# A hybrid attention and convolution layer on one core: sixteen convolution blocks regrouped as Strassen products ahead of the attention

## The chip, the core and the metric

The kernel runs on one core of one Trainium2 chip. TensorE does the matmuls, VectorE, ScalarE and GpSimd do the elementwise work, and SyncE issues nearly all transfers. In the rows these are PE, DVE, ACT, POOL and SP; PEld is the weight load of PE. The metric is the device time of one execution in microseconds, as the median of several runs; one profiled execution gives the rows.

## What is computed

One decoder layer in float32, 1024 positions and 16 learned meta positions ahead of them, width 1024. A normalised input is projected to 4104 columns; half of them feed softmax attention, the other half a gated convolution of width 3; both branches are normalised per head or group, gated, and go through one output projection.

```python
def _hybrid_layer(h, norm_g, w_in, b_f, conv_w, attn_norm_g, conv_norm_g, w_out):
    u = _rmsnorm(h, norm_g)
    proj = jnp.einsum('bld,de->ble', u, w_in)
    q, k, v, f_logit, z_attn, gate_b, gate_c, xc, z_conv = jnp.split(proj, SPLIT_POINTS, axis=-1)
    log_f = jax.nn.log_sigmoid(f_logit + b_f)
    cum_logf = jnp.cumsum(log_f, axis=1)
    attn = _fox_attention(q.reshape(shp), k.reshape(shp), v.reshape(shp), cum_logf)
    y_attn = _group_rmsnorm(attn, attn_norm_g, ATTN_HEADS) * jax.nn.silu(z_attn)
    conv = _causal_depthwise_conv(gate_c * xc, conv_w)
    y_conv = _group_rmsnorm(gate_b * conv, conv_norm_g, CONV_GROUPS) * jax.nn.silu(z_conv)
    mix = jnp.concatenate([y_attn, y_conv], axis=-1)
    return h + jnp.einsum('ble,ed->bld', mix, w_out)
```

The attention has 8 heads of 64 and a causal mask; its logits are q.k/8 plus the difference of the summed log forget gates. A last normalisation follows the layer.

## The kernel before

**Numbers in two parts.** Each float32 operand of a large matmul is held as a rounded part `hi` and the rest `lo`, and each product is three matmuls: hi by hi, lo by hi, hi by lo. To split a tensor takes one copy (ScalarE, or GpSimd for weights in `hi_pool`, L112) and one subtraction (VectorE, `lo_vec`, L115).

**Input and q (L211 to L250).** Eight row tiles of the transposed input `xs` and of the q weights are loaded, split, and multiplied for the four q blocks at once (L232, 192 matmuls of 512 columns into eight PSUM tiles). The input isn't normalised over its tokens first: only the gain `gnt` is applied. The factor of each token, `rbc`, is found beside this from a second load of the input (`ht`, L249, squares on ScalarE) and is multiplied in wherever a projection leaves PSUM (L275, L297, L451, L472, L478 and so on).

**k and v (L165, L324).** Two k blocks, then v with the forget gate (L324, 260 columns a matmul, two PSUM tiles for each of nine token tiles), then two k blocks. A block is 128 output columns: 8 input tiles by 3 matmuls for each chunk of positions. q, k and v go to DRAM in parts and come back head by head (`load_head`).

**Filler and attention.** The 16 convolution blocks (gates c, x, b and zc in four groups) and the four z gates of the attention are cut into steps of three matmuls, in the list `filler`. The attention is cut into stages, one for each head and half of its queries: `s_step` (scores, row maximum on VectorE, exponential on ScalarE), `s_end` (the small chain of GpSimd, ScalarE and VectorE that merges the maxima, then the scaling of the probabilities `pn` on GpSimd, L635), `t_step` (transposes on TensorE, copy `ph` on ScalarE, subtraction `pl` on VectorE), `v_step` (L669) and `fold`. While a stage transposes and multiplies one half, it already does the scores of the next. `weave` sets TensorE's order: it puts filler steps between the attention's, in proportion to the matmul time left, with a start of `HEAD` us of filler before the first scores. Every matmul of this part is `pinned` to that order; the other engines' order is chosen by the compiler's scheduler.

**Finish.** `norm` and `silu` finish a branch; the output projection (L788, 360 matmuls, most of 512 columns) reads the branches back from DRAM (`yd`), adds the input and applies the last norm.

Of the kernel before, what the change touches and what calls it, by code (L numbers as in the profile page):

```python
# [22 lines left out]
KT = 8  # L23
# [12 lines left out]
def hybrid_kernel(ctx, tc, hT, h, w_q, w_vf, w_m, w_o, gn, bf, cw, ga, gc, gf, out):  # L36
# [37 lines left out]
    rtok = const.tile([P, 9], F32, name="rtok")  # L74
    rbc = const.tile([P, L], F32, name="rbc")
    r2bc = const.tile([P, L], F32, name="r2bc")

# [18 lines left out]
    FIN = (4, 12)  # L96
    FIN3 = (8, 1)
# [21 lines left out]
    wp = xctx.enter_context(tc.tile_pool(name="wp", bufs=2, side=R_SIDE))  # L119
# [6 lines left out]
    order = [0, 1, 2, 3]  # L126
    for i in range(4):
        order += [4 + 4 * i, 5 + 4 * i, 7 + 4 * i] + ([20 + i, 6 + 4 * i] if i < 3 else [6 + 4 * i, 20 + i])
    staged, ready = {}, {}

    def load_w(m):
        staged[m] = wp.tile([P, KT, P], F32, name="wm", bufs=1)
        ins = nc.sync.dma_start(staged[m], w_m[m].rearrange("p (k c) -> p k c", k=KT))
        if m < 4:
            behind(ins)

    def split_w(m):
        ws = staged.pop(m)
        whi = wp.tile([P, KT, P], F32R, name="wmhi")
        wlo = wp.tile([P, KT, P], F32R, name="wmlo")  # L140
        hi_pool(whi, ws)
        lo_vec(wlo, ws, whi)
        ready[m] = whi, wlo

    def block_steps(m, chunks, psum, done):

        at = order.index(m)
        nxt = order[at + 1] if at + 1 < len(order) else None
# [28 lines left out]


    with ExitStack() as ca:
# [3 lines left out]
        kp = ca.enter_context(tc.tile_pool(name="kp", bufs=2))  # L183
        qk = ca.enter_context(tc.tile_pool(name="qk", bufs=1))
        st = ca.enter_context(tc.tile_pool(name="st", bufs=2))
        sm = ca.enter_context(tc.tile_pool(name="sm", bufs=1))

        ones = sm.tile([P, P], F32, name="ones")
        nc.gpsimd.memset(ones, 1.0)
        tri = sm.tile([P, P], F32, name="tri")  # L190
# [6 lines left out]
        nc.vector.tensor_copy(blk, blk32)  # L197

# [4 lines left out]
        for i in range(8):  # L203
            nc.tensor.matmul(pw, zero[:, :P], zero, start=True, stop=True)


        psq = [[(psx if (m, c) == (3, 1) else ps1).tile([P, 512], F32, name="px" if (m, c) == (3, 1) else "ps")
                for c in range(2)] for m in range(4)]
        with ExitStack() as c1:
            wq = c1.enter_context(tc.tile_pool(name="wq", bufs=3))  # L210
            for k in range(KT):  # L211
                ws = wq.tile([P, 512], F32, name="ws")
                xs = wq.tile([P, L], F32, name="xs")
                whi = wq.tile([P, 512], F32R, name="wqhi")
                wlo = wq.tile([P, 512], F32R, name="wqlo")
                if k == 0:
                    behind(nc.sync.dma_start(xs[:, :528], hT[:, 0, :528]))
                behind(nc.sync.dma_start(ws, w_q[k * P:(k + 1) * P, :]))
                (nc.vector.tensor_copy if k == 0 else nc.scalar.copy)(whi, ws)
                for a, b in ((0, 528), (528, L)) if k == 0 else ((0, L),):  # L220
                    if a or k:
                        behind(nc.sync.dma_start(xs[:, a:b], hT[:, k, a:b]))
                    nc.scalar.activation(xhi[k][:, a:b], xs[:, a:b], AF.Copy, scale=gnt[:, k:k + 1])
                    nc.vector.scalar_tensor_tensor(xlo[k][:, a:b], xs[:, a:b], gnt[:, k:k + 1], f(xhi[k][:, a:b]),
                                                   ALU.mult, ALU.subtract)
                lo_vec(wlo, ws, whi)
                todo = [(m, n, c) for m in range(4) for n in range(3) for c in range(2)]
                if k == 0:
                    todo.sort(key=lambda t: t[1:])
                for m, n, c in todo:  # L230
                    wt, xt = ((whi, xhi[k]), (whi, xlo[k]), (wlo, xhi[k]))[n]
                    nc.tensor.matmul(psq[m][c], wt[:, m * P:(m + 1) * P], xt[:, NM + 512 * c:NM + 512 * c + 512],  # L232
                                     start=(k == 0 and n == 0), stop=(k == KT - 1 and n == 2))
            load_w(0)
            split_w(0)
            for t, v in ((bft, bf.broadcast_to([P, HEADS])), (cwt, cw), (gat, ga), (gct, gc)):
                behind(nc.sync.dma_start(t, v))
            qraw = [[qk.tile([P, 512], F32, name=f"qraw{m}{c}") for c in range(2)] for m in range(4)]
            for m in range(4):
                nc.scalar.copy(qraw[m][0], psq[m][0])  # L240
                nc.vector.tensor_copy(qraw[m][1], psq[m][1])


            ss = sm.tile([P, 9], F32, name="ss")
            nc.vector.memset(ss, 1.0)
            for j in range(9):
                n = P if j < 8 else NM
                ht = st.tile([P, D], F32, name="ht")
                behind(nc.sync.dma_start(ht[:n], h[j * P:j * P + n, :]))  # L249
                nc.scalar.activation(ht[:n], ht[:n], AF.Square, accum_out=ss[:n, j:j + 1])  # L250
# [16 lines left out]
        def k_done(m):  # L267
# [4 lines left out]
            def done(c, ps):  # L272
# [5 lines left out]
                if c == 2:  # L278
                    nc.sync.dma_start(kd[m][0], f(kh))
                    nc.sync.dma_start(kd[m][1], f(kl))  # L280
# [627 lines left out]
```

## Time and profile before

| | us |
|---|---|
| median of 3 runs | 595.03 (594.82 to 595.29) |
| profiled execution, its own time | 596.83 |
| span in the profile | 595.1 |
| last k block ends, filler begins | 149.6 |
| first scores of the attention | 167.7 |
| last value matmul of the attention | 490.9 |

The span is what lies between the first and the last instruction; 1.7 us of the profiled execution lie around it, and the median run is 1.8 us shorter than the profiled one. Busy time of PE counts matmuls whose ends are modelled and overlap, so how long one matmul holds the engine is read from the distance of their starts, for which the chain of waits serves: it lists runs of matmuls on PE with their count.

### The profile page before, as it was taken

Reading aid. Unit: us, or ns where it says so; the run is one execution under the profiler, and the core shown is the slowest. Engines: PE = TensorE matmul, PEld = TensorE weight load, DVE = VectorE, ACT = ScalarE, POOL = GpSimd, SP = SyncE. Lnnn points to the kernel's source line nnn. Section 1 sums busy time; section 2 is a strip of 40 time slices with the busy share of each in tenths; the row PEclk is TensorE's granted clock in tenths of the full one; section 3 lists DMA queues with packets and bytes.
Section 4 is the critical chain, followed back from the end, with each engine's and each line's share of the span. In section 5 each row is a group of like instructions: output and inputs, shape, how many; then the busy total and the mean of one; then the engine's idle time right before and its main releaser. Section 6 shows DMA issues by size and latency. Waiting matters only on the chain.

```text
span 595.1 us, 9156 instructions
## 1 busy us (share of the span) xinstructions
PE 578.0 (97%) x3230; PEld 509.6 (86%) x3230; DVE 377.9 (64%) x834; ACT 285.4 (48%) x667; POOL 168.0 (28%) x290
## 2 busy tenths in 40 slices
PE   9999999999998999999999999999999999899995
PEld 6888999999997889988879997889998887688884
DVE  5415851133367686879776888868869777947432
ACT  5355431131044575556764655747636676705221
POOL 1002010121027244151243254430552416710000
PEclk9999999999999999999999999999999999899999
DMA  8764594249811605415126134251350227453201
GB/s 287 237 194 141 195 341 142 70 147 280 262 39 36 144 35 135 120 57 155 44 75 143 71 108 112 75 143 37 111 197 16 73 88 243 171 205 113 100 35 70
DMA packets 35221, 78.14 MB, mean 131 GB/s; under 512 B 4024, under 2 KB 13384, under 8 KB 35176
## 3 DMA queue, kind: packets, MB, share of 16 engines
q1 hardware_dynamic: 35032, 77.57, 41.6%
q8 instruction: 25, 0.41, 0.3%
q14 instruction: 20, 0.16, 0.1%
q10 hardware_dynamic: 144, 0.00, 0.0%
HBM read 55.92 MB, written 21.64 MB: 130 GB/s over the span
## 4 chain that ended last, share of the span: by engine, by line
PE 71%; DMA 10%; DVE 6%; POOL 4%; ACT 3%; issue 3%; SPq 2%; POOLq 0%; ACTq 0%; DVEq 0%
PE pj L165 30%; PE ps L324 8%; PE p L788 8%; PE pt L645 5%; PE po L669 5%; PE pj L788 4%; PE ps L165 4%; DMA k<-kd 3%; DMA ht<-in_h 3%; PE pn L605 3%; PE pn L606 3%; DMA xs<-in_hT 2%; DVE mlo L115 2%; POOL pn L635 1%; DMA wm<-in_w_m 1%
## 5 line engine op out<-in xcount | busy, mean ns | idle before, releaser
L165 PE MATMUL pj<-xhi,wmhi 128*128 128x512 f32 (+1 forms) x384 | 144.9, 377 | 1.0 <-DVE kf L275 0.5
L165 PE MATMUL pj<-xhi,wmlo 128*128 128x512 f32 (+1 forms) x384 | 137.1, 357 | 0.0
L165 PE MATMUL pj<-xlo,wmhi 128*128 128x512 f32 (+1 forms) x384 | 136.8, 356 | 0.0
L613 ACT ACTIVATE pn<-pn,nmx 128x328 f32<-128x328 f32 (+6 forms) x112 | 60.5, 541 | 52.7 <-DVE nmx L612 27.9
L165 PEld LDWEIGHTS pj<-xhi,wmlo 128*128 128x128 f32 x384 | 72.2, 188 | 8.4
L165 PEld LDWEIGHTS pj<-xhi,wmhi 128*128 128x128 f32 x384 | 72.6, 189 | 6.2 <-issue 1.4
L165 PEld LDWEIGHTS pj<-xlo,wmhi 128*128 128x128 f32 x384 | 72.8, 190 | 3.8
L654 ACT CAST ph<-pt 128x512 fp32r<-128x512 f32 (+4 forms) x112 | 49.6, 445 | 51.0 <-PE po L669 23.3
L635 POOL TENSOR_SCALAR pn<-pn,fc 128x328 f32<-128x328 f32 (+4 forms) x112 | 69.3, 639 | 1.6
L115 DVE TENSOR_TENSOR pl<-pt,ph 128x512 fp32r<-128x512 f32 (+1 forms) x96 | 54.6, 572 | 20.2 <-ACT ph L654 19.5
L112 POOL TENSOR_SCALAR wmhi<-wm 128x1024 fp32r<-128x1024 f32 x24 | 26.2, 1093 | 141.2 <-DMA wm<-in_w_m 81.8
L645 PE MATMUL pt<-ident,pn 128*128 128x128 f32 x288 | 47.4, 273 | 3.9 <-POOL pn L635 2.2
L645 PEld LDWEIGHTS pt<-ident,pn 128*128 128x128 f32 x288 | 36.3, 140 | 14.4 <-POOL pn L635 3.6
L115 DVE TENSOR_TENSOR wmlo<-wm,wmhi 128x1024 fp32r<-128x1024 f32 x24 | 29.4, 1223 | 18.0 <-POOL wmhi L112 17.9
L609 DVE CUSTOM_DVE_ANT_0 pn<-pn,maskn 128x328 f32<-128x328 f32 (+3 forms) x64 | 31.9, 500 | 11.0 <-PE pn L606 9.3
L669 PE MATMUL po<-ph,v 128*128 128x512 f32 (+4 forms) x112 | 37.0, 336 | 0.0
L605 PE MATMUL pn<-k,q 128*128 128x328 f32 (+6 forms) x112 | 36.6, 328 | 0.1
L606 PE MATMUL pn<-k,q 66*128 66x328 f32 (+6 forms) x112 | 36.1, 322 | 0.0
L669 PE MATMUL po<-pl,v 128*128 128x512 f32 (+1 forms) x96 | 33.2, 350 | 0.0
L788 PE MATMUL p<-whi,mlo 128*128 128x512 f32 (+1 forms) x77 | 30.2, 392 | 2.4 <-DVE mlo L115 2.4
L165 PE MATMUL ps<-xhi,wmhi 128*128 128x346 f32 (+1 forms) x96 | 31.0, 323 | 1.1 <-ACT qraw L240 1.1
L612 DVE TENSOR_REDUCE nmx<-pn 128x1 f32<-128x346 f32 (+4 forms) x48 | 24.8, 521 | 9.6 <-PE pn L606 9.6
(227 smaller groups left out, 1229.5 us busy)
## 6 DMA issues: line engine op xcount, KB each, us to landing
wm<-in_w_m SPq DMA_DIRECT2D x24, 512.0 KB, 3.8
k<-kd SPq DMA_DIRECT2D x24, 260.0 KB, 5.3
q<-qd SPq DMA_DIRECT2D x24, 256.0 KB, 5.9
vd<-vv SPq DMA_DIRECT2D x9, 512.0 KB, 2.9
v<-vd SPq DMA_DIRECT2D x8, 576.0 KB, 6.5
ht<-in_h SPq DMA_DIRECT2D x8, 512.0 KB, 5.6
yd<-gy SPq DMA_DIRECT2D x16, 256.0 KB, 2.8
q<-in_w_o SPq DMA_DIRECT2D x8, 512.0 KB, 4.5
```

The lines of the kernel that those rows point to most:

```text
L115: nc.vector.tensor_tensor(lo, src, f(hi), ALU.subtract)
L165: ins = nc.tensor.matmul(ps[:, :w], wt[:, k, :], xt[:, t0:t0 + w], start=(k == 0 and n == 0), stop=(k == KT - 1 and n == 2))
L324: nc.tensor.matmul(ps[c][:P if n == P else 48, :260], x[k][:, ts_] if n == P else x[:, k, :], w[k][:, 260 * c:260 * c + 260], start=(k == ...
L605: pinned(nc.tensor.matmul(ps[:, :w], q1[:, qs], k1[:, ks], start=True, stop=False))
L606: pinned(nc.tensor.matmul(ps[:, :w], q2[:DH + 2, qs], k2[:DH + 2, ks], start=False, stop=True))
L609: nc.vector.tensor_tensor_reduce(ps[:, :w], ps[:, :w], maskn[:, MASKW - w:], op0=ALU.add, op1=ALU.min, scale=-1.0, scalar=-NEG, accum_out= ...
L613: nc.scalar.activation(pn[j][:, ks], ps[:, :w], AF.Exp, bias=nmx[c][at], scale=-1.0 if last else 1.0, accum_out=smx[c][at])
L635: nc.gpsimd.tensor_scalar(pn[j][:, k0:k0 + w], pn[j][:, k0:k0 + w], fc[:, j % 4, i:i + 1], 1.0, ALU.mult, ALU.mult)
L645: pinned(nc.tensor.transpose(pt[:, q0:q0 + P], pn[j][:, ks], ident))
L654: nc.scalar.copy(ph[:, at:], pt[:, at:])
L669: pinned(nc.tensor.matmul(po[:, at:], v2[:, vk, :], t[:, at:], start=(kt == 0 and i == 0), stop=(kt == 4 * c + 4 and i == len(parts) - 1)))
L788: ins = nc.tensor.matmul(held[n][:, :w], a[:, tt], b[:, cs], start=(e == ORDER[0] and i == 0), stop=(e == ORDER[-1] and i == 2))
```

## The change

**Order.** q, then v, then the four k blocks, then all 16 convolution blocks, then the start of the z gates, then the attention. Only the rest of the z gates stays as filler (`HEAD` is 4.0 in place of 15.75).

**Normalised input.** `ht` isn't loaded any more. The squares are taken from `xs` on ScalarE, summed over tiles on GpSimd, and over partitions by a matmul with ones; the result is turned into `rbc`. Then `x_norm` rewrites all of `xs`, `xhi` and `xlo` with the normalised input, in two halves of positions. The eighth q tile has no PSUM tile during the loads and is computed after the sums.

```diff
+            def x_norm(k, a, b):
+                nc.vector.scalar_tensor_tensor(xs[k][:, a:b], xs[k][:, a:b], gnt[:, k:k + 1], rbc[:, a:b],
+                                               ALU.mult, ALU.mult)
+                nc.scalar.copy(xhi[k][:, a:b], xs[k][:, a:b])
+                lo_vec(xlo[k][:, a:b], xs[k][:, a:b], xhi[k][:, a:b])
...
+            for k in range(KT):
+                x_norm(k, 0, 528)
+            q_done(0, 0)
+            q_done(0, 1)
+            for k in range(KT):
+                x_norm(k, 528, L)
+                if k < 6:
+                    q_done(*((1, 0), (1, 1), (2, 0), (2, 1), (3, 0), (3, 1))[k])
```

`q_done` takes a q tile out of PSUM (a multiplication by `rbc` on VectorE), splits and stores it. The nine pairs of v tiles use the same seven PSUM buffers that hold the q tiles until then.

**Strassen.** Two neighbouring blocks of one kind form a pair: 256 output columns by 1024 inputs by 1024 (or 1026) positions, cut in halves each way. Seven products of quarters take the place of eight: 12 matmuls over 512 positions each (kinds zc and b), or 24 over 258 and 256 (kinds c and x). The sums of input quarters are made once (`x_sum`, 20 sums, GpSimd adds, ScalarE and VectorE split) beside the k blocks. The sums of weight quarters are made for each product (`w_sum`, three products ahead). Each product is copied into, added to or taken from one or two quarters of the result in SBUF.

```diff
+    MGOES = {1: (("11", "="), ("22", "=")), 5: (("11", "-"), ("12", "=")), 3: (("12", "+"), ("22", "+")),
+             2: (("22", "-"), ("21", "=")), 4: (("21", "+"), ("11", "+")), 6: (("22", "+"),), 7: (("11", "+"),)}
...
+            if len(MSUMS[m]) > 1:
+                t = sbp[0].tile([P, 4, P], F32, name="wst", bufs=1)
+                nc.gpsimd.tensor_tensor(t, one, quads[p, MSUMS[m][1]], MSUMS[m][2])
+                one = t
+            nc.scalar.copy(hi, one)
+            lo_vec(lo, one, hi)
...
+            for t0, w in ((0, 258), (258, 256)) if pairs[p][0] in "cx" else ((2, 512),):
+                ps = psumj()
+                for k in range(4):
+                    xh, xl = x_part(m, k)
+                    for i, (wt, xt) in enumerate(((hi, xh), (hi, xl), (lo, xh))):
+                        pinned(nc.tensor.matmul(ps[:, :w], wt[:, k, :], xt[:, t0:t0 + w],
+                                                start=(k == 0 and i == 0), stop=(k == 3 and i == 2)))
+                o = t0 if pairs[p][0] in "cx" else 0
+                for q, how in MGOES[m]:
+                    d = outp[place[p]][:, int(q[0]) - 1, int(q[1]) - 1, o:o + w]
+                    if how == "=":
+                        nc.scalar.copy(d, ps[:, :w])
+                    else:
+                        nc.vector.tensor_tensor(d, d, ps[:, :w], ALU.add if how == "+" else ALU.subtract)
```

**Into the attention.** The first 14 of the 64 z steps follow the last product and cover the last norms; then the buffers of the convolution are given up, the attention's take their place, and `load_head(0)` is issued.

```diff
+    for n in range(Z_HEAD):
+        filler.pop(0)[1]()
+        due(len(prods) + n // 4)
+    due(10 ** 6)
+    due(10 ** 6)
+    bctx.close()
+    fctx.close()
...
-    HEAD = 15.75
+    HEAD = 4.0
```

On PE, where q ends and the next projection begins. Before, the first k block (`wmhi`) follows the last q matmul:

```order
L232 MATMUL px<-xhi_121,wqlo 128x512
L165 MATMUL ps<-xhi_107,wmhi 128x348
L165 MATMUL ps<-xlo_108,wmhi 128x348
L165 MATMUL ps<-xhi_107,wmlo 128x348
L165 MATMUL ps<-xhi_109,wmhi 128x348
```

Now three sums over partitions (`onesr`) and the eighth q tile (`w3hi`, 24 matmuls) come first, then v (`wvhi`); the brackets name the engine on whose semaphore a matmul waits:

```order
L334 MATMUL px<-sq,onesr 128x346
L341 MATMUL px<-xhi_101,w3hi 128x512 [waits DVE_49]
...
L341 MATMUL px<-xhi_115,w3lo 128x512
L391 MATMUL ps<-wvhi_180,xhi_101 128x256 [waits DVE_49,Activation_49]
L391 MATMUL ps<-wvlo_188,xhi_101 128x256
L391 MATMUL ps<-wvhi_180,xlo_102 128x256
L391 MATMUL ps<-wvhi_181,xhi_103 128x256 [waits Activation_49]
...
L391 MATMUL ps<-wvhi_187,xlo_116 128x264
L391 MATMUL ps<-wvhi_180,xhi_101 128x256 [waits DVE_49]
```

The first matmul of the first v tile waits for VectorE, and the matmuls that read the eight `xlo` don't wait for it again; the second v tile waits for VectorE once more.

On DVE at the same place, in the order in which VectorE runs them now:

```order
L335 TENSOR_SCALAR sa<-px 128x346
L359 SCALAR_TENSOR_TENSOR xs<-xs,gnt,rbc 128x528 x8
L110 TENSOR_TENSOR xlo_102<-xs,xhi_101 128x528
...
L110 TENSOR_TENSOR xlo_116<-xs,xhi_115 128x528
L85 SCALAR_TENSOR_TENSOR rbc<-xTrueu,xTruet 128x346
L349 SCALAR_TENSOR_TENSOR qf<-ps,rbc 128x512 x2
L359 SCALAR_TENSOR_TENSOR xs<-xs,gnt,rbc 128x512 x8
L110 TENSOR_TENSOR ql<-qf,qh 128x512 x2
...
L349 SCALAR_TENSOR_TENSOR qf<-ps,rbc 128x512
```

The first `qf` frees the PSUM tile of the first v tile; it stands behind all sixteen operations of the first half of `x_norm`. The third `qf` (last row) frees that of the second v tile, and stands behind the sixteen of the second half but one.

On PE in the attention. Before, convolution steps (`pj<-xhi,wmhi`) stand between nearly any two steps of the attention (`pt`, `pn`, `po`):

```order
L645 MATMUL pt<-ident,pn_1620 128x128
L165 MATMUL pj<-xhi_107,wmhi 128x342
L165 MATMUL pj<-xlo_108,wmhi 128x342
L165 MATMUL pj<-xhi_107,wmlo 128x342
L165 MATMUL pj<-xhi_109,wmhi 128x342
L165 MATMUL pj<-xlo_110,wmhi 128x342
L165 MATMUL pj<-xhi_109,wmlo 128x342
L605 MATMUL pn<-k_1944,q_1942 128x264
```

Now the attention's steps mostly follow each other, each with its own wait, and a z step comes once in a while:

```order
L156 MATMUL pj<-xhi_113,wmhi 128x512
L156 MATMUL pj<-xlo_114,wmhi 128x512
L156 MATMUL pj<-xhi_113,wmlo 128x512
L732 MATMUL pn<-k_4174,q_4172 128x392
L733 MATMUL pn<-k_4175,q_4173 128x392
L772 MATMUL pt<-ident,pn_3722 128x128 [waits PE_49,Pool_49]
...
L732 MATMUL pn<-k_4174,q_4172 128x392 [waits Activation_49]
L733 MATMUL pn<-k_4175,q_4173 128x392
L732 MATMUL pn<-k_4174,q_4172 128x456 [waits Activation_49]
```

What moved is the cover: 16 convolution blocks stood among these rows, and of the 64 z steps 50 are left for them.

## Rows read from the trace of the kernel before

**Rows 1.** The page, busy time of each engine, its share of the span, instructions.

```profile
PE 578.0 (97%) x3230; PEld 509.6 (86%) x3230; DVE 377.9 (64%) x834; ACT 285.4 (48%) x667; POOL 168.0 (28%) x290
```

**Rows 2.** Busy time by stretch: us, then each engine (instructions), clock, DMA share, GB/s.

```profile
core 0: us, PE busy (x) PEld busy (x) DVE busy (x) ACT busy (x) POOL busy (x), PEclk, DMA share, GB/s
4.80:50.00 45.20, 45.20 (x193) 36.22 (x192) 16.63 (x18) 22.89 (x33) 2.82 (x6) 1.00 0.73 247
149.60:491.00 341.40, 336.78 (x1889) 297.98 (x1889) 254.67 (x616) 192.03 (x488) 123.96 (x222) 1.00 0.34 99
250.00:310.00 60.00, 58.47 (x317) 50.12 (x316) 49.07 (x120) 38.60 (x97) 23.05 (x43) 1.00 0.30 87
190.00:470.00 280.00, 277.33 (x1562) 245.02 (x1560) 218.64 (x535) 166.53 (x426) 105.78 (x193) 1.00 0.34 95
491.00:595.10 104.10, 94.53 (x426) 77.20 (x424) 60.07 (x102) 40.61 (x85) 23.98 (x9) 0.97 0.38 134
```

**Rows 3.** The chain that ended last, in order of time: start, length, what, count.

```profile
66.25 9.43 PE ps L165 x58
75.68 49.79 PE ps L324 x415
187.56 1.39 PE pj L165 x6
227.54 0.95 PE pj L165 x6
```

**Rows 4.** Groups of PE by form, counts of convolution and z matmuls (one of three passes).

```profile
L165 PE MATMUL pj<-xhi,wmhi 128*128 128x512 f32 x192 | 80.9, 421 | 0.0
L165 PE MATMUL pj<-xhi,wmhi 128*128 128x342 f32 x192 | 64.0, 333 | 1.0 <-DVE kf L275 0.5 <-DVE cx L451 0.3
```

**Rows 5.** Groups of VectorE: busy us, mean ns of one, idle before.

```profile
L115 DVE TENSOR_TENSOR pl<-pt,ph 128x512 fp32r<-128x512 f32 (+1 forms) x96 | 54.6, 572 | 20.2 <-ACT ph L654 19.5
L609 DVE CUSTOM_DVE_ANT_0 pn<-pn,maskn 128x328 f32<-128x328 f32 (+3 forms) x64 | 31.9, 500 | 11.0 <-PE pn L606 9.3 <-ACT pn L613 1.2
L115 DVE TENSOR_TENSOR wmlo<-wm,wmhi 128x1024 fp32r<-128x1024 f32 x24 | 29.4, 1223 | 18.0 <-POOL wmhi L112 17.9
L612 DVE TENSOR_REDUCE nmx<-pn 128x1 f32<-128x346 f32 (+4 forms) x48 | 24.8, 521 | 9.6 <-PE pn L606 9.6
L651 DVE STREAM_TRANSPOSE pt<-pn 32x32 f32<-32x32 f32 x64 | 13.4, 216 | 2.3
L681 DVE TENSOR_TENSOR o<-po,otmp 64x512 f32<-64x512 f32 x16 | 11.0, 686 | 3.8 <-ACT otmp L680 3.6
L609 DVE DVE_READ_ACCUMULATOR2_ANT nmx<- 128x1 f32 x64 | 8.5, 133 | 0.2
L436 DVE SCALAR_TENSOR_TENSOR otmp<-zc,otmp 128x512 f32<-128x512 f32 x8 | 5.7, 714 | 0.9 <-ACT e L622 0.5 <-ACT otmp L435 0.3
```

**Rows 6.** Groups of ScalarE in the attention.

```profile
L613 ACT ACTIVATE pn<-pn,nmx 128x328 f32<-128x328 f32 (+6 forms) x112 | 60.5, 541 | 52.7 <-DVE nmx L612 27.9 <-DVE nmx L609 24.0
L654 ACT CAST ph<-pt 128x512 fp32r<-128x512 f32 (+4 forms) x112 | 49.6, 445 | 51.0 <-PE po L669 23.3 <-DVE pt L651 13.4 <-PE pt L645 7.8
```

**Rows 7.** VectorE in order of time: four operations in one run, and one alone.

```profile
63.02 2.49 DVE L297 SCALAR_TENSOR_TENSOR qraw<-qraw,rbc 128x512 f32<-128x512 f32 x4
510.32 0.68 DVE L438 TENSOR_TENSOR zs<-zs,otmp 128x512 f32<-128x512 f32 x1
```

**Rows 8.** VectorE and GpSimd in order of time, near 497 us.

```profile
497.93 2.88 DVE L438 TENSOR_TENSOR zs<-zs,otmp 128x512 f32<-128x512 f32 x1
496.89 3.38 POOL L552 TENSOR_TENSOR wlo<-q,whi 128x1024 fp32r<-128x1024 f32 x1
505.09 2.42 POOL L552 TENSOR_TENSOR wlo<-q,whi 128x1024 fp32r<-128x1024 f32 x1 [4.82 <-ACT whi L549]
```

**Rows 9.** The chain again: the transfers of the first head, and the scaling ahead of its transposes.

```profile
132.54 7.72 DMA k<-kd
183.45 2.27 POOL pn L635 x4
```

**Rows 10.** Busy time by stretch at the only stall over 2 us after the start.

```profile
514.70:517.30 2.60, 0.49 (x3) 0.10 (x1) 2.60 (x2) 2.60 (x4) 2.33 (x2) 1.00 0.25 97
517.30:521.00 3.70, 3.70 (x10) 2.88 (x11) 3.70 (x2) 0.86 (x1) 3.70 (x2) 0.54 0.77 272
```

More of the change, by code (lines that the diff above doesn't have):

```diff
@@ new lines, in hybrid_kernel, with load_quads, w_sum @@
+    quads, wsum = {}, {}
+    sbp = [None]
+    def load_quads(p, which):
+        if p < len(pairs):
+            kind, g = pairs[p]
+            for q in which:
+                i, j = int(q[0]) - 1, int(q[1]) - 1
+                quads[p, q] = sbp[0].tile([P, 4, P], F32, name="wquad", bufs=6)
+                src = w_m[BASE[kind] + 4 * (g + i)].rearrange("p (k c) -> p k c", k=KT)
+                nc.sync.dma_start(quads[p, q], src[:, 4 * j:4 * j + 4, :])
+    def w_sum(n):
+        if n < len(prods):
+            p, m = prods[n]
+            hi = sbp[0].tile([P, 4, P], F32R, name="wsh")
+            lo = sbp[0].tile([P, 4, P], F32R, name="wsl")
+            one = quads[p, MSUMS[m][0]]
+            if len(MSUMS[m]) > 1:
[4 more added lines that the diff above has]
+            lo_vec(lo, one, hi)
+            wsum[n] = hi, lo
@@ L204, in hybrid_kernel @@
             nc.tensor.matmul(pw, zero[:, :P], zero, start=True, stop=True)
[L207 to L250, printed above, removed]
@@ new lines, in due @@
+    def due(n):
+        for t in [t for t in pend if t[0] <= n]:
+            pend.remove(t)
+            t[1]()
+    KINDS = ("c", "x", "zc", "b")
+    place = (0, 1, 2, 1, 1, 0, 2, 0)
+    with tc.tile_pool(name="pb", bufs=8, space=PSUM, reuse_waits="tile") as pb:
+        psumj = lambda: pb.tile([P, 512], F32, name="pb")
+        for n, (p, m) in enumerate(prods):
+            due(n)
+            first = prods[n][1] == MORDER[0]
+            if first and p:
+                load_quads(p + 1, QUADS[:2])
+            w_sum(n + AHEAD_W)
+            if m == MORDER[3]:
+                load_quads(p + 1, QUADS[2:])
+            hi, lo = wsum.pop(n)
+            for t0, w in ((0, 258), (258, 256)) if pairs[p][0] in "cx" else ((2, 512),):
[10 more added lines that the diff above has]
+                        nc.scalar.copy(d, ps[:, :w])
+                    else:
+                        nc.vector.tensor_tensor(d, d, ps[:, :w], ALU.add if how == "+" else ALU.subtract)
+            if m in MENDS:
+                quarter_done(n, p, MENDS[m])
@@ L420, in tick @@
+    NORM_LAG = 6.1
+    norms, open_norm = [], []
     def tick(x):
@@ L480, in z_done @@
+                zsil[i] = zsp.tile([P, S], F32, name="zs")
+            z = zsil[i][:, 512 * c:512 * c + 512]
+            nc.scalar.copy(z, ps)
+            silu(z)
             if c == 1:
```

475 lines of the change are left out of this document (275 added, 200 removed).

## The prediction

> **What bounds the kernel now.** I read the page's busy times first: PE is busy 97% of the span and no other engine above 64% [rows 1]. That number hides where the others would bind, so the table by stretch came next. From 149.6 to 491.0 us, where convolution, z gates and attention are woven, PE is busy 336.8 of 341.4 us at full clock, while VectorE reaches 78% over 190 to 470 us and 82% in the fullest 60 us [rows 2]. Then I read the chain for what one matmul costs PE: 9.43/58 = 0.163 us for 346 columns (k), 49.79/415 = 0.120 for 260 (v), 1.39/6 = 0.232 for 512 and 0.95/6 = 0.158 for 342 [rows 3]; in the q stretch it is 45.2/193 = 0.234 [rows 2]. The last reading is how PE comes to be full. The groups by form give three passes of 192 matmuls of 342 columns and of 192 of 512 [rows 4]. Of the latter, 48 a block make eight convolution and four z blocks. So the filler is 576 x 0.158 + 576 x 0.232 = 225 us, of which convolution is 91 + 89 = 180. The woven stretch without it is 341.4 - 225 = 117 us, idle time and norms included: what the attention costs PE. The filler is what the attention's waits hide behind.
>
> **What the change takes away.** Products of pairs c and x: 4 pairs x 7 products x 24 matmuls = 672 at 0.120 us (258 and 256 columns, taken as 260) = 80.6. Pairs zc and b: 4 x 7 x 12 = 336 x 0.232 = 78.0. Together 158.6 in place of 180: **21 us less for PE**. This gain is sure; the rest of the sum asks what becomes of it.
>
> **The front, up to the end of k.** Loads of `ht` go, but PE was full there, so that gives nothing. Now q is 168 matmuls x 0.234 = 39.3 from 4.8, to 44.1. The sums over partitions use one PSUM tile three times, each time emptied by VectorE, which by its order still has four v-weight subtractions and one `wmlo` (1.22 us [rows 5]) to do, behind transfers. I put 5.5 us on this, with ends 2 and 8. The eighth q tile is 24 x 0.234 = 5.6 us.
>
> Then v can't start: its first matmul waits for a PSUM tile that the first `qf` frees, and by the order of VectorE 8 multiplications and 8 subtractions of 528 stand ahead of it. Back to back such an operation costs 2.49/4 = 0.62 us [rows 7]. From the start of the eighth q tile VectorE has the rest of the inverse root (7 small operations, some 3.5 us), 16 x 0.62 = 9.9, and the `qf` 0.6, or 14 us; PE has 5.6 to do meanwhile and stands for about 9. The second v tile waits in the same way: 19 operations x 0.62 = 11.8 against 48 x 0.120 = 5.8 of matmuls, 6 more. After that v and k run as before: 49.9 and 288 x 0.163 = 46.9. End of k: 44.1 + 5.5 + 5.6 + 9 + 49.9 + 6 + 46.9 = **167 us**, where it was 149.6. So 17 of the 21 us are spent here. PE's clock is at risk too: at the one stall of 2.6 us with hardly a matmul, the granted clock of the next 3.7 us was 0.54, ten matmuls in place of sixteen [rows 10]. Here that costs little, because the first v tile, slowed down, only uses up the second stall.
>
> **The products.** 158.6, and 12 norm matmuls x 0.232 = 2.8. VectorE in four pairs (81 us of PE): 76 operations of 512 at 0.62 and 32 of 257 at some 0.4 (an estimate between 0.62 and half of it) = 60 us. GpSimd's adds come on top. A `zs` product of VectorE took 2.88 us while a GpSimd add ran, against 0.68 alone [rows 7, 8]; the add itself takes 2.42 for 1024 columns when undisturbed, so about 1.2 for 512. There are 24 in four pairs, 29 us. If VectorE waited for all of them it would need 89 us, 8 more than PE, 16 over both halves; if for none, nothing is lost. I take 3, since eight PSUM tiles let VectorE lag by some products and the c pairs let it catch up. End of the products: 167 + 158.6 + 2.8 + 3 = 331. [...]
>
> **Into the attention.** 14 z steps x 0.7 = 9.7, then `HEAD` lets about 7 steps pass, 4.9: PE has work to 346. The first head's loads stand behind the last norm's store in SyncE's queue, and its buffers are the convolution's; I put the issue at 340 (the norm's eight operations and the lag). Before, the last of them to matter was issued at 132.5 and landed 7.7 us later [rows 9]; with those issued ahead of it that is about 10. First scores at **350 us**.
>
> **The attention, the main term.** PE's share is at most 117 + 50 z steps x 0.7 = 152 us. VectorE's: `pl` 54.6, maxima 31.9 + 24.8 + 8.5, corner transposes 13.4, `fold` 11.0 [rows 5], about 32 operations of norms and gates x 0.71 = 23, three `wmlo` 3.7: 171 us by durations. Those overlap (0.684 listed, 0.62 back to back), so 171 x 0.91 = **155 us**, smaller groups left out. ScalarE is close: 60.5 + 49.6 [rows 6], 16 copies of `fold`, and the four activations of each gate and norm, some 145. So VectorE becomes the bound, with ScalarE just behind, and each waits for the other inside every step (`pl` for `ph`, exponential for maximum). How full can VectorE be? The ends are 1.0 (155 us) and the 0.78 that it had with PE as the bound (199); the nearest row is its fullest 60 us, 0.82, and I take that: 189. To it I add 8 us at the start, where VectorE idles between the first maxima and the first transposes (GpSimd's chain and four scalings, 2.27 us [rows 9]). Last value matmul: 350 + 8 + 189 = 547; before, 490.9. The output part isn't touched: 104.1 us [rows 2]. **Sum: 651 us.**
>
> The profiled execution took 596.83 with a span of 595.1; the median run is 1.8 below the former, so the span's sum is compared with the median as it is: 651 against 595.03, 9% slower. A measurement of this kernel can tell about 0.2% from no change.
>
> **Rivals.**
> 1. *PE's clock falls in the attention.* The row after the 2.6 us stall shows that idle time can bring it down; against it, in the woven stretch, 99% busy, it never fell [rows 2]. If half of PE's 152 us ran at the lower level, they would become 228 and PE would bind: 350 + 8 + 228 + 104 = 690, or more. [...] Chance 0.12.
> 2. *VectorE fills without gaps.* The attention then takes 155, the products lose nothing and the waits at the sums are at their lower end: 350 - 6 + 8 + 155 + 104 = 611. For it: of its idle time some 19 us ahead of the maxima were waits for PE [rows 5]. Against: as many ahead of `pl` were waits for ScalarE, which is nearly as full. Chance 0.11.
> 3. *Faster: VectorE is cheaper in a full queue than its rows say.* It sets the front's two waits, the products' lag and the attention alike, so one cause would lift all three. At 0.62 of the cost shown, the waits of 15 us become 4, the lag goes, and the attention is PE's 152 without the 8: 339 - 3 + 152 + 104 = 592. That is the point from which it decides; the run of four in a row (0.62 against 0.684) shows 0.91 and no more. Chance 0.04.
>
> **How the numbers follow.** The forecast, VectorE-bound attention with the front's waits, has 0.73. Its unknowns: the fill (189 within 155 to 199, the small groups upward), the sums (2 to 8), the lag (0 to 16), the load. Range 618 to 682; beyond it lie rivals 1 and 3 and part of 2. Faster by over 0.2% is rival 3 and a little of the unknown, 0.05; slower 0.93; within 0.2%, 0.02.
>
> **What would show it.** After the eighth q tile PE should stand for some 9 us until `qf`, and for about 6 before the second v tile; k should end near 167, the products near 331 with PE nearly full, the first scores stand near 350. From there VectorE should be over 80% busy and PE near 75%, `ph` and `pn` waiting for VectorE. The forecast is wrong if the attention takes near 150 us with PE full, if the granted clock is low there, or if v starts right after the eighth q tile.

## The result, and the profile after

The changed kernel takes **728.48 us** (median of four runs, 724.65 to 732.98) beside 595.16 for the kernel before (four runs, 594.82 to 596.29): a ratio of 1.2239, 95% interval 1.2160 to 1.2317. The forecast was 651 us with a range of 618 to 682. The sign was right and the time lies far outside. The profiled execution took 724.65 us, the shortest of the four, with a span of 722.9, so the rows below account for 72 of the 77 us above the forecast.

First the page of the changed kernel: busy time, share and instructions of each engine [rows 1], then busy tenths of PE in 40 slices of the span and the clock granted to it.

```profile
PE 614.1 (85%) x3275; PEld 519.0 (72%) x3275; DVE 490.8 (68%) x998; ACT 361.7 (50%) x814; POOL 265.2 (37%) x344
...
PE   9955799997999968999788778678777777799996
...
PEclk9996799998999988999888799899999998999999
```

PE has fewer columns to multiply and is nevertheless busy for 614.1 us in place of 578.0, and no other engine is fuller: the next one, VectorE, has 68%. The clock row, all nines before but for one eight near the end, has dips from the fourth slice to the end of the attention.

Next the table by stretch of the changed kernel, which answers to [rows 2]: q; sums and eighth q tile and the wait for v; v; k; products; z head; attention; output.

```profile
core 0: us, PE busy (x) PEld busy (x) DVE busy (x) ACT busy (x) POOL busy (x), PEclk, DMA share, GB/s
4.80:46.90 42.10, 39.93 (x167) 31.10 (x168) 31.05 (x33) 24.73 (x38) 19.17 (x7) 1.00 0.51 170
47.10:73.10 26.00, 9.94 (x31) 6.98 (x30) 21.93 (x38) 10.04 (x19) 1.47 (x2) 0.72 0.14 41
73.10:130.60 57.50, 54.37 (x416) 54.17 (x417) 25.73 (x55) 17.14 (x34) 14.11 (x17) 0.92 0.45 146
130.60:183.40 52.80, 48.99 (x295) 48.22 (x294) 43.19 (x51) 20.58 (x41) 34.32 (x24) 0.94 0.40 128
183.40:373.10 189.70, 173.84 (x1022) 153.20 (x1021) 138.81 (x212) 86.00 (x162) 74.52 (x56) 0.94 0.17 57
373.10:390.20 17.10, 16.24 (x70) 12.66 (x68) 9.21 (x12) 9.26 (x15) 4.68 (x16) 1.00 0.59 156
390.20:621.20 231.00, 173.93 (x850) 134.95 (x849) 162.72 (x495) 149.91 (x419) 89.32 (x199) 0.91 0.37 98
621.20:722.90 101.70, 93.38 (x426) 76.52 (x425) 56.88 (x99) 41.86 (x86) 25.00 (x9) 0.99 0.37 135
```

Against the forecast: k ends at 183.4, not 167 (+16.4); the products take 189.7, not 164 (+25.7); from there to the first scores 17.1, not 19 (-1.9); the attention 231.0, not 8 + 189 = 197 (+34); the output part 101.7, not 104.1 (-2.4). That adds up to +71.8, and 651 + 71.8 = 722.8 is the span but for rounding. Against the kernel before: the front is 183.4 - 149.6 = 33.8 us longer, the products are new with 189.7, and the attention is only 323.4 - 231.0 = 92.4 us shorter, though all its convolution matmuls are gone.

Where PE waited in the products and in the attention, from the view of waits (engine, waiting group, what ended the wait: us in total, times, longest), products first:

```profile
PE pb L506 <- ACT gsh L501: 13.0, 5, 4.4
PE pb L507 <- DVE gsl L110: 2.0, 4, 0.8
```

```profile
PE pt L772 <- DVE pl L110: 18.5, 20, 2.3
PE pt L772 <- POOL pn L762: 15.6, 10, 4.6
PE po L796 <- DVE ph L110: 7.2, 9, 2.6
PE pn L732 <- ACT pn L740: 6.2, 11, 0.9
```

In the products 15.0 of its 15.9 us of idle time stand at the two norm matmuls. In the attention it waits for three engines in turn, seldom long. In the kernel before, PE had hardly a wait in the attention and was busy for all but 4.3 us of it:

```profile
PE pt L645 <- POOL pn L635: 2.2, 2, 1.5
PE pt L645 <- DVE pl L115: 1.4, 2, 0.8
```

```profile
167.70:491.10 323.40, 319.14 (x1780) 280.57 (x1779) 249.07 (x607) 191.21 (x486) 121.97 (x220) 1.00 0.32 93
```

The groups of the other two engines are no dearer than before [rows 5, 6] (`pl` 573 ns in place of 572, `ph` 448 in place of 445), and these two waited for each other before too: `pl` 21.8 us for `ph` (19.5 before), `ph` 15.2 us for the corner transposes (13.4 before). What is new is that PE waits for them:

```profile
L781 ACT CAST ph<-pt 128x512 fp32r<-128x512 f32 (+4 forms) x112 | 48.9, 448 | 44.0 <-DVE pt L778 15.2
...
L110 DVE TENSOR_TENSOR pl<-pt,ph 128x512 fp32r<-128x512 f32 (+1 forms) x96 | 53.7, 573 | 22.8 <-ACT ph L781 21.8
```

### The profile page after: what moved, and what is told of

The parts are those of the page before. It is cut to its first block, busy times and chain, and to the rows that moved or that the text cites. A ratio compares the mean times of both kernels' runs of the same rounds, so it can differ in the third digit from the quotient of the medians.

```text
span 722.9 us, 9839 instructions
## 1 busy us (share of the span) xinstructions
PE 614.1 (85%) x3275; PEld 519.0 (72%) x3275; DVE 490.8 (68%) x998; ACT 361.7 (50%) x814; POOL 265.2 (37%) x344
## 5 line engine op out<-in xcount | busy, mean ns | idle before, releaser
L212 POOL TENSOR_TENSOR wst<-wquad 128x512 f32<-128x512 f32 x40 | 54.6, 1365 | 99.7 <-DVE wsl L110 91.6
L781 ACT CAST ph<-pt 128x512 fp32r<-128x512 f32 (+4 forms) x112 | 48.9, 448 | 44.0 <-DVE pt L778 15.2
L110 DVE TENSOR_TENSOR pl<-pt,ph 128x512 fp32r<-128x512 f32 (+1 forms) x96 | 53.7, 573 | 22.8 <-ACT ph L781 21.8
L583 DVE TENSOR_TENSOR dst<-dst,pb 128x258 f32<-128x258 f32 (+2 forms) x96 | 45.9, 505 | 19.3 <-PE pb L575 18.9
L214 ACT CAST wsh<-wst 128x512 fp32r<-128x512 f32 x40 | 24.7, 618 | 51.8 <-POOL wst L212 31.2
L732 PE MATMUL pn<-k,q 128*128 128x328 f32 (+6 forms) x112 | 44.6, 402 | 7.0 <-ACT pn L740 6.2
L575 PE MATMUL pb<-xs,wsh 128*128 128x258 f32 (+2 forms) x192 | 45.7, 333 | 0.0
L110 DVE TENSOR_TENSOR wsl<-wst,wsh 128x512 fp32r<-128x512 f32 x40 | 33.0, 825 | 16.1 <-ACT wsh L214 15.8
L391 PE MATMUL ps<-wvhi,xhi 128*128 128x264 f32 (+1 forms) x128 | 30.5, 301 | 10.4 <-DVE qf L349 10.4
L575 PEld LDWEIGHTS pb<-xs,wsh 128*128 128x128 f32 x192 | 33.5, 197 | 3.3
L732 PEld LDWEIGHTS pn<-k,q 128*128 128x128 f32 x112 | 22.8, 203 | 17.6 <-ACT pn L740 16.4
L439 POOL TENSOR_TENSOR t<-xs 128x514 f32<-128x514 f32 x20 | 29.2, 1467 | 15.4 <-DVE c1l L110 4.9
L739 DVE TENSOR_REDUCE nmx<-pn 128x1 f32<-128x346 f32 (+4 forms) x48 | 24.4, 515 | 13.3 <-PE pn L733 13.2
```

Of the source, the lines that this page charges most:

```text
L110: nc.vector.tensor_tensor(lo, src, f(hi), ALU.subtract)
L212: nc.gpsimd.tensor_tensor(t, one, quads[p, MSUMS[m][1]], MSUMS[m][2])
L575: pinned(nc.tensor.matmul(ps[:, :w], wt[:, k, :], xt[:, t0:t0 + w], start=(k == 0 and i == 0), stop=(k == 3 and i == 2)))
L583: nc.vector.tensor_tensor(d, d, ps[:, :w], ALU.add if how == "+" else ALU.subtract)
L732: pinned(nc.tensor.matmul(ps[:, :w], q1[:, qs], k1[:, ks], start=True, stop=False))
L781: nc.scalar.copy(ph[:, at:], pt[:, at:])
```

## The experiments

Two theories stood for the attention, the largest term. **Clock**: PE falls to half clock in its waits, and that makes the attention long. **Handoffs**: PE, ScalarE, VectorE and GpSimd pass each tile to each other, the time between is what the filler had covered, and the clock is only a sign of it. For the front and the products the question was what PE waits behind. Each kernel was timed against the kernel before; lengths of stages are from one profiled execution.

### The convolution first, nothing else

```diff
 # the kernel before
+    conv_time = sum(x for x, _ in filler)
+    for gate in gates:
+        filler += gate
...
-    HEAD = 15.75
+    HEAD = conv_time + 13.0
```

> The kernel before with its 16 plain convolution blocks ahead of the attention (their weights loaded in that order) and only the z gates left as cover in it; no Strassen products, no normalized input, order q, k, v as before. Theory cover (the attention alone costs what it costs in the changed kernel, 231 us, whatever stands ahead of it): 150 to the end of the front + 180 for the blocks + 5 to 17 to the first scores + 231 + 102 = 668 to 680, so some 50 of the 130 us that the change costs lie in the Strassen products and the new front. Rival (it is the products' backlog that spoils the attention): the attention here takes 200 or less, in all 640 or less.

Measured: 683.4 us, ratio 1.1494 (1.1462 to 1.1525). Blocks and attention by stretch:

```profile
149.60:336.00 186.40, 184.24 (x981) 166.35 (x981) 88.09 (x109) 38.35 (x61) 27.27 (x34) 1.00 0.22 72
349.30:580.90 231.60, 177.34 (x853) 137.09 (x851) 168.62 (x504) 149.94 (x417) 90.35 (x199) 0.89 0.32 87
```

The attention takes 231.6 us here, with no product, no normalised input and the old order ahead of it. That is what the theory of cover gave, with the whole kernel 3 us above its range. So 88 of the 133 us come from taking the convolution out of the attention. The rest lies ahead of it: the front (33.8), the way to the first scores (17.1 in place of 13.3) and what the products cost above plain blocks. The blocks end near 336, some 186 us behind the front, so the products, 21 us shorter on paper, took 3 us more than the blocks they replace.

### How much cover does the attention need?

One number each: `HEAD = 105.0` in the kernel before, and `HEAD = 150.0` in the kernel of the last section.

> The kernel before with one number changed: the filler work put ahead of the first scores is 105 of its planner's units in place of 15.75 (205 in all), so that of the 196 us of filler matmuls in the attention about 99 are left. Theory surplus (the attention goes at the larger of two paces: 231 us by its handoffs, or its own 125 us of TensorE work and the filler): 125 + 99 = 224 is just under 231, so the kernel takes 600 to 608. Rival (every us of cover that goes costs its share: a line from 595 with 196 us of cover to 683 with 28): about 646.

> The kernel with all convolution blocks first in the filler, and 150 units ahead of the first scores in place of 177, which leaves about 57 us of filler in the attention in place of 28. Theory surplus: the attention stays at 231 us and takes 29 us of filler for nothing, so 683 falls by 29 to 650 to 658. Rival (the line): 668.

Measured: 643.64 us (ratio 1.0784, 1.0729 to 1.0840) and 670.61 (1.1258, 1.1190 to 1.1327). I had expected 600 to 608 and 650 to 658; what came is close to the rival's 646 and 668. The stretch of the attention in the first and in the second:

```profile
265.90:539.30 273.40, 239.14 (x1293) 205.30 (x1292) 204.64 (x550) 164.52 (x442) 107.43 (x208) 0.95 0.33 91
```

```profile
317.30:563.60 246.30, 197.28 (x981) 155.78 (x980) 180.08 (x521) 160.83 (x437) 92.95 (x202) 0.94 0.32 86
```

The table splits each attention from PE's side. What PE loses at half clock is taken as half of the busy time that lies in the stretches with a granted clock of 0.50, an estimate and a little much: in the changed kernel matmuls of 512 columns start 0.42 to 0.43 us apart near 59 us, where the granted clock is 0.50, and 0.23 apart near 65, where it is 1.00. The matmuls at full clock are the rest of its busy time.

| kernel | filler matmuls in the attention | its length, us | matmuls at full clock, us | lost at half clock, us | PE idle in it, us |
|---|---|---|---|---|---|
| before | 1030 | 323.4 | 319.1 | 0 | 4.3 |
| `HEAD` 105 | 547 | 273.4 | 227.0 | 12.2 | 34.3 |
| convolution first, 150 | 244 | 246.3 | 183.1 | 14.2 | 49.0 |
| convolution first | 118 | 231.6 | 156.5 | 20.8 | 54.3 |
| changed | 118 | 231.0 | 155.0 | 19.0 | 57.1 |

The first 483 matmuls that go take 92 us of PE's time with them and shorten the attention by 50. So the attention isn't the larger of two paths, as I had twice assumed: from the first matmuls taken out, between two fifths and a half of the time freed come back as waits and slow matmuls. From the first row to the last, 164 us of matmuls go, and 53 come back as waits and 19 as slow matmuls. The cover had no surplus. Why the rest of the filler doesn't run into the waits is not shown; that it stands in a fixed order between steps, and not where the waits are, would explain it.

### Is it the clock?

One matmul of zeros into the open value sum ahead of 96 value steps; it adds nothing to the result:

```diff
 # the changed kernel
+        if kt > 0:
+            for _ in range(1):
+                pinned(nc.tensor.matmul(po..., zc16, zc16..., start=False, stop=False))
```

> The changed kernel with one more matmul of zeros (128 x 512) into the open sum ahead of 96 of the value steps, which adds nothing to the result and 96 x 0.22 = 21 us of TensorE work. Theory clock (the attention takes 231 us because TensorE falls to half clock in its gaps): the granted clock of the attention rises from 0.89 to over 0.95 and the time falls by 15 to 25 us. Theory handoffs (the attention goes at the pace of what TensorE, ScalarE and VectorE hand to each other, the clock is only a symptom): the clock rises, and the time stays within 6 us or grows by up to 21.

Measured: 736.42 us, 1.2390 (1.2359 to 1.2420); the attention 240.2 at a clock of 0.90 (231.0 at 0.91 without). The work was added, and the clock stayed, though both theories had it rise: the matmuls had been put ahead of the value matmuls, which wait 9 us in all in the changed kernel, and not ahead of the transposes, which wait 38. It tells only that 96 matmuls between the steps cost 9 us. So the zeros went ahead of the transposes, with a control:

```diff
 # the changed kernel; the control has the last change alone, from 3 to 2
+        for _ in range(2):
+            pinned(nc.tensor.matmul(junk..., zc16, zc16..., start=True, stop=True))
         pt = pst.tile([P, 512], F32, name="pt")
...
-    psn = cp.enter_context(tc.tile_pool(name="psn", bufs=3, space=PSUM, reuse_waits="tile"))
+    psn = cp.enter_context(tc.tile_pool(name="psn", bufs=2, space=PSUM, reuse_waits="tile"))
```

> The changed kernel with two matmuls of zeros (128 x 512) ahead of the transposes of each of the 112 value tiles, where TensorE's largest gaps stand; they write a PSUM tile of their own that nobody reads, and the scores have two PSUM tiles in place of three for it. 224 x 0.22 = 49 us of TensorE work that nothing waits for, into gaps of 57. Compared with the run that has the two score tiles alone. Theory clock: the half-clock time in the attention falls from 44 us to under 15, and the time by 10 to 20 us against the control. Theory handoffs: the clock rises likewise, but the time stays within 5 us of the control or above it, since the matmuls of zeros delay as much as the clock gives back.

> The control: the changed kernel with two PSUM tiles for the scores in place of three, nothing else. Theory handoffs: a tile less makes TensorE wait for ScalarE's exponentials more often, 3 to 15 us more than the changed kernel. Theory clock: within 3 us of it.

Measured: 751.38 us (1.2581, 1.2532 to 1.2630) with the zeros, 748.85 (1.2570, 1.2523 to 1.2617) without. The attention with the zeros, then that of the control:

```profile
390.80:647.60 256.80, 217.24 (x1075) 146.71 (x1074) 166.80 (x495) 153.65 (x419) 87.88 (x199) 0.93 0.33 88
```

```profile
391.40:647.50 256.10, 195.95 (x851) 150.75 (x851) 165.91 (x495) 153.50 (x419) 89.60 (x199) 0.81 0.33 88
```

Taken as a mix of 1.00 and 0.50, the two levels in the changed kernel's trace, a mean of 0.81 over 256.1 us means (1 - 0.81)/0.5 x 256.1 = 97 us at half clock, and 0.93 means 36. Sixty us of half clock went, and the attention is 256.8 in place of 256.1. The same split shows why this doesn't say that the clock is worth nothing:

| kernel | length, us | matmuls at full clock | lost at half clock | PE idle |
|---|---|---|---|---|
| changed | 231.0 | 155.0 | 19.0 | 57.1 |
| control, two score tiles | 256.1 | 154.3 | 41.7 | 60.1 |
| with zeros | 256.8 | 201.0 | 16.2 | 39.6 |
| norms later | 232.5 | 154.4 | 26.1 | 52.0 |
| weights behind the sums | 231.7 | 155.5 | 24.0 | 52.1 |
| both | 233.4 | 154.1 | 26.8 | 52.5 |

(The last three kernels are those of the last two experiments; their attention is that of the changed kernel.) The zeros cost 47 us of matmuls, took 25 off what the clock takes and 20 off the waits. So the run can't tell what the clock alone would give, and no run raises it alone. The control shows how the clock enters: one PSUM tile fewer for the scores makes the attention 25 us longer, and 23 of these are slower matmuls, only 3 more waiting. The whole kernel is 20 us longer, more than the 3 to 15 that I expected. The last three rows show that waits and clock trade: PE lost 5 to 8 us more to the clock than in the changed kernel and idled 5 less, so the attention is only 1 to 2 us longer. Between executions of one kernel the clock does go with the time: those of the changed kernel have spans of 722.9, 724.9, 728.6 and 731.3 us at a mean clock of 0.930, 0.928, 0.923 and 0.917. So both theories hold in part: in the changed kernel's attention the waits are the larger share (57 us) and the clock the smaller (19), and part of what the clock takes is made up by shorter waits. How much of it would come back at full clock is not shown.

### A tile more for the transposes

```diff
 # the control
-    pst = cp.enter_context(tc.tile_pool(name="pst", bufs=2, space=PSUM, reuse_waits="tile"))
+    pst = cp.enter_context(tc.tile_pool(name="pst", bufs=3, space=PSUM, reuse_waits="tile"))
```

> The changed kernel with two PSUM tiles for the scores and three for the transposes, in place of three and two. Against the control with two and two (749 us): theory transposes (the wait for a tile that VectorE's remainder has to leave, 12.9 us in the control, is what a tile more takes away): 730 to 740. Rival (the tile comes free sooner but VectorE and ScalarE are no further): 745 or more, and TensorE's wait for the exponentials' tiles stays at 19 us.

Measured: 738.62 us, 1.2422 (1.2376 to 1.2467). PE's waits in the attention, in the control and then here:

```profile
PE pn L732 <- ACT pn L740: 18.8, 28, 1.1
PE pt L772 <- POOL pn L762: 13.3, 9, 3.4
PE pt L772 <- DVE pl L110: 12.9, 14, 2.4
PE po L796 <- DVE ph L110: 5.6, 7, 2.4
```

```profile
PE pn L732 <- ACT pn L740: 18.4, 25, 1.0
PE pt L772 <- POOL pn L762: 17.5, 12, 3.4
...
PE pt L772 <- DVE pl L110: 1.0, 1, 1.0
```

The wait of the transposes for a tile that `pl` has to leave is all but gone, from 12.9 to 1.0, as the theory had it; the wait for the exponentials' tiles stays, as its rival had it, and that for GpSimd's `pn` grows by 4.2. The attention falls from 256.1 to 242.5 us, of which 11 are waits (60.1 to 48.9), and the mean clock in it stays at 0.81. So one kind of handoff, the reuse of a PSUM tile, costs 10 us of the kernel's time, with the clock as low as before. The four pools of the attention hold eight PSUM tiles (3, 2, 1 and 2 in the changed kernel); a split with three for both wasn't run.

### Less work for VectorE

```diff
 # the changed kernel
-        pl = pp.tile([P, 512], F32R, name="pl")
...
-            lo_vec(pl[:, at:], pt[:, at:], ph[:, at:])
-            box[kt] = at, kt, (ph, pl)
+            box[kt] = at, kt, (ph,)
```

> The changed kernel without the remainder of the probabilities in the value sums: 96 VectorE subtractions of 0.57 us and 96 matmuls of 0.37 are left out of the attention, and the output is that much coarser. Theory handoffs (VectorE with its waits sets the pace): the attention falls from 231 us to 180 to 205 and the kernel to 678 to 703, while TensorE's granted clock in it does not rise. Theory clock: TensorE's gaps grow, its clock falls further, and the attention stays above 215.

Measured: 703.09 us, 1.1798 (1.1749 to 1.1847). The attention:

```profile
391.20:598.90 207.70, 159.87 (x755) 121.83 (x754) 116.37 (x399) 148.55 (x419) 91.51 (x199) 0.88 0.40 109
```

It is 23.3 us shorter, just above what handoffs with VectorE as the pace would give and below what the clock theory would (the kernel's time, 703.1, is on the edge likewise). The edit takes out three things at once: VectorE's subtractions (162.7 - 116.4 = 46 us of its busy time), the 96 matmuls that read their results, and the wait of a PSUM tile for `pl`. By the split, PE's matmuls at full clock fall from 155.0 to 138.4 us, its waits from 57.1 to 47.8, and the clock takes 2.5 more. So 17 of the 23 us are PE's own work, and 46 us less for VectorE took 9 us of waits away. VectorE is at 56% now, ScalarE at 72%, and PE still waits, most of all for GpSimd:

```profile
PE pt L772 <- POOL pn L762: 19.2, 11, 4.4
```

So VectorE alone isn't the pace of this stage. That no single engine is, and that the round trip of a tile through all four is what counts, fits this and the extra tile; it isn't shown by itself.

### The norm later, the weights behind the sums

```diff
 # the changed kernel, norms later
-            pend.append((n + 1, lambda: pend.append((n + 2, go()))))
+            pend.append((n + 3, lambda: pend.append((n + 4, go()))))
```

> The changed kernel with the square of each convolution output 3 products behind it, in place of 1, and its two norm matmuls 4 products behind, in place of 2. Theory place (TensorE waits for gsh because the matmuls stand too early in its order): the stalls of 1 to 5 us at the norm matmuls go, the products take 165 to 172 us in place of 189.6, in all 17 to 25 us less. Rival (VectorE and ScalarE have fallen behind by themselves): the stalls stand later or at the accumulators, the products still take 183 or more.

```diff
 # the changed kernel, the loop over v's weights put behind the sums
+                    if k >= 4:
+                        after(cast, marks[0])
+                        after(lo, marks[1])
...
```

> The changed kernel with the casts and remainders of the last four tiles of v's weights put behind the reciprocal roots on ScalarE and VectorE. Theory place (the sums over partitions waited behind weights that had not landed): the sums take about 6 us in place of 11, the first v matmul comes 5 to 9 us earlier than 73.1, and the end falls by 5 to 10. Rival: the remainders then come too late for v's first tile, and the first v tile ends no earlier.

Norms later: 721.29 us, 1.2128 (1.2102 to 1.2155). The products and the z head:

```profile
183.40:354.40 171.00, 164.85 (x1020) 147.22 (x1018) 132.84 (x205) 81.16 (x157) 75.85 (x56) 0.99 0.17 59
354.40:384.10 29.70, 18.55 (x70) 13.93 (x70) 15.88 (x21) 13.49 (x23) 4.68 (x16) 0.91 0.41 117
```

The products take 171.0 as the place theory said, 18.7 less, and the clock is at 0.99. That is nearly their whole excess: by the split they were 163.4 us of matmuls, 10.4 lost at half clock and 15.9 idle, and are 163.3, 1.5 and 6.1. Then two thirds are given back: the way to the first scores takes 29.7 in place of 17.1. The reason stands in SyncE's queue (start, length):

```profile
366.96 9.63 SPq L547 DMA_DIRECT2D yd<-gy  x3
376.69 0.52 SPq L712 DMA_DIRECT2D q<-qd  x1
```

The three last stores wait for their norms, the loads of the first head stand behind them, and PE waits 5.84 us for `k`; another 3.56 it waits for VectorE behind the last product.

Weights behind the sums: 721.99 us, 1.2141 (1.2110 to 1.2172), 6.5 less than the changed kernel, though the two intervals overlap by a little and the spans differ by only 3.1. The sums take 3.9 us (47.9 to 51.8) in place of 11.1, and v starts at 67.5 in place of 73.1; but v takes 61.6 us in place of 57.5, since PE idles 6.2 us in it in place of 3.1 and the clock is 0.90 in place of 0.92, and k ends only 1.5 us earlier. So the place theory holds for the sums; most of what it gave was eaten by v.

### Both

> The changed kernel with the remainders of v's last weights behind the reciprocal roots, as in the run with that alone, and with the norms of the first four quarters 3 and 4 products behind, those of the last four 2 and 3. The two gains lie in different stages and add up: 6 us in front, 10 to 19 in the products, 702 to 712 in all. Rival: what comes earlier out of the front waits again ahead of the first scores or at k, and the time stays above 715.

Measured: 715.75 us, 1.2009 (1.1952 to 1.2067), 4 above the range that I gave and just over the bound of the rival. The products take 172.6; the way to the first scores 24.7. The front ends at 184.3, no earlier than in the changed kernel (183.4): as the rival had it, what the sums gain was gone by the end of k. It is the fastest form of the change that computes the whole result, and 20% slower than the kernel before. No run points to a version that beats the kernel before.

## Why the prediction was wrong

**What held.** The products' own matmuls: 161.4 us forecast, 163.4 by the split, and 20.8 less than those of the plain blocks (184.2). PE's own work in the attention: at most 152 forecast, 155.0 by the split. That no saving of 21 us can pay for the lost cover. PE stood for `qf` at both v tiles, 7.3 us (9 forecast) and 3.1 (6 forecast). The head and the output part were right within 2.4 us, the head by luck: I had PE out of work and waiting for the first loads, and it was busy for 16.2 of the 17.1 us.

**The front, 16.4 us over.** PE's matmuls at full clock ahead of the products are 143.2 us in both kernels; the 33.8 us more are 23.6 of waits and 10.2 of half clock. Of the 16.4 that I missed, 3.0 lie in q, which ended at 47.1 in place of 44.1 (1.8 of them a wait for VectorE's `wqlo`), 5.6 in the sums, 1.6 in v and 5.9 in k.

**"I put 5.5 us on this, with ends 2 and 8" (the sums).** 11.1 us, 47.1 to 58.2. Named rightly, sized wrongly: VectorE's emptying of the first tile stood behind the last four subtractions of v's weights, and those waited for transfers. VectorE in order of time in the changed kernel (start, length, what; in brackets the idle time before and what ended it):

```profile
47.37 1.50 DVE L110 TENSOR_TENSOR wvlo<-wvs,wvhi 128x520 fp32r<-128x520 f32 x2 [1.44 <-ACT wvhi L317]
51.55 0.70 DVE L110 TENSOR_TENSOR wvlo<-wvs,wvhi 128x520 fp32r<-128x520 f32 x1 [2.69 <-ACT wvhi L317]
53.18 0.70 DVE L110 TENSOR_TENSOR wvlo<-wvs,wvhi 128x520 fp32r<-128x520 f32 x1 [0.93 <-ACT wvhi L317]
53.80 0.51 DVE L335 TENSOR_SCALAR sa<-px 128x348 f32<-128x348 f32 x1
```

I had counted the operations and not the arrival of what they read. In the run with the weights behind the sums they took 3.9, within my ends.

**"Here that costs little" (the clock in the front).** 0.72 from 47.1 to 73.1, 0.92 in v, 0.94 in k: by the split 4.8 us lost in v and 2.6 in k. The eighth q tile, 5.6 us in my sum, took 7.4. And k had waits that I didn't have: 2.2 us for a `wmhi` of GpSimd and 1.6 for a `wmlo` of VectorE, which stood behind the sums of input quarters on GpSimd and the splits of them on VectorE.

**"If VectorE waited for all of them ... I take 3" (the products' lag).** 28 us. I compared VectorE's total with PE's over a pair, as a bound by throughput. VectorE was 73% busy, and PE waited for it at a product only once, for 0.9 us; what waited were the norm matmuls, pinned two products behind a quarter's end while the chain to them (gate, square, cast, subtraction) went through ScalarE and VectorE in order. The first stall and what followed it, by stretch:

```profile
255.90:260.30 4.40, 0.01 (x1) 0.01 (x1) 4.33 (x8) 3.72 (x8) 2.62 (x2) 0.98 0.31 94
260.30:267.00 6.70, 6.19 (x14) 4.52 (x15) 4.04 (x6) 2.78 (x5) 1.97 (x2) 0.51 0.15 55
```

4.4 us idle, then 6.7 at a granted clock of 0.51, where PE is the bound and 3.3 us are lost. Moving only the norms took most of the stalls (15.9 us to 6.1) and of the slow matmuls (10.4 us lost to 1.5) away together.

**"So VectorE becomes the bound ... I take 0.82" (the attention, the main term).** 162.7 us of VectorE in 231.0, or 0.70, outside the ends 0.78 and 1.0 of my term. The step failed as reasoning, not only in size. The fill of 0.82 came from a stretch in which PE, full of filler, was busy for 58.5 of 60 us [rows 2] and hardly ever waited; with the filler gone that premise was gone too. By the prediction's own prices PE needs 117 + 118 x 0.232 = 144 us and VectorE 155; the attention takes 231, which is neither. My 8 + 189 left PE 45 us of waits beside 152 of work and nothing for the clock; it had 57 of waits, 155 of work and 19 lost at half clock. The runs with a tile less, a tile more and without `pl` move the attention by +25, -14 and -23 us, and the line over four amounts of filler shows that some two fifths of the cover had stood in waits or kept the clock up.

**Rival 1 (the clock) is half of it.** The clock did fall: to 0.72 at the sums, 0.92 in v, 0.94 in k and in the products, and 0.91 over the 231 us of the attention, which means 42 us at half speed beside 57 idle. The lower level that the rival priced at half speed is in the trace of the kernel before too: granted 0.50 from 517.5 to 520.5 us, inside the stretch of 0.54 in [rows 10]. But the rival's price was wrong: it had half of PE's work in the attention at the lower level and PE bound, 76 us more; 38 of PE's 174 busy us there lay at half clock, which is 19 lost. With 10 in the front and 10 in the products that makes 40 of the 72 us above the forecast, a term that the sum put at nothing or little. It is a count of slow matmuls and not what a full clock would give: in the rows above, waits were 5 us longer where the clock took 5 to 8 less. Where PE does bind, in the products, waits and clock went together. Rivals 2 (VectorE without gaps) and 3 (faster) fell: VectorE's group means in the attention are unchanged (`pl` 573 ns beside 572, the maxima 501 and 515 beside 500 and 521).

## What to carry to other kernels

Work that stands in another stage's waits has no price of its own there: before moving it out, find what the stage costs alone. One run of the old kernel with the work ahead of it (683 us here) would have told two thirds of the outcome. Busy shares don't bound a stage in which four engines pass small tiles on through few buffers: there, count the round trip and its tiles, since here VectorE, the fullest helper, was at 0.70 and PE at 0.75, and the stage took 231 us where a bound by either gave 155. Split PE's time into matmuls, half clock and waits before calling the clock a cause or a sign: here it was a part of the price. And a matmul pinned into a dense stage has to stand behind the whole chain that feeds it, while transfers for the next stage must not queue behind that chain's stores.

## What the runs showed of the hardware

In the changed kernel the granted clock of the 6.7 us after the wait of 4.4 us was 0.51; with 57 us of waits in the attention, the longest 4.6, its mean was 0.91, and with 60 us, in the control, 0.81. At a granted clock of 0.50 matmuls of 512 columns came 0.42 to 0.43 us apart, at 1.00 0.23. With half of the busy time at 0.50 counted as lost, the six attentions with the same matmuls come out alike, 152.3 to 155.5 us of them, though 38 to 83 us of their busy time lay there. Adding 96 matmuls between the steps left the mean at 0.90, beside 0.91; adding 224 in the longest waits raised it from 0.81 to 0.93, at a cost of 47 us of matmuls. And in the changed kernel VectorE's subtraction `wsl`, with both inputs in SBUF, took 1.16 us on average in the 18 of 56 cases in which it overlapped an operation of GpSimd, and 0.69 in the other 38. With the other VectorE operations of the products whose tensor inputs are both in SBUF that makes some 20 us, by the same comparison, where I had put 16 as the upper end. The additions `dst<-dst,pb` read one input from PSUM and took the same either way: 0.42 us for 256 and 258 columns, 0.68 for 512.
